# A gated conv block on one core: y_b's scalings ordered behind y_a's last evacuation, and T2 built pair by pair between the FFN's first products

## The chip, the core and the metric

The kernel runs on one core of one Trainium2 chip. The time is the device time of one execution in microseconds; lower is better. The core has a matrix engine (TensorE, PE in the profile), two elementwise engines (VectorE, DVE; ScalarE, ACT), a third (GpSimd, POOL), and a queue that issues loads (SyncE, SP). Each engine takes its instructions in the order that was compiled; an instruction that waits holds up all behind it on its engine.

## The reference

One layer of 1024 channels over 1024 time steps, all float32:

```python
h = rms_norm(x, norm_mix_g) * (1 + sc1) + sh1
b_s, c_s, v_s, v_c, gl_c, gate_br = split(h @ w_in)
y_a = (b_s * causal_dwconv3(c_s * v_s)) @ w_short_out
u = causal_dwconv31(v_c * sigmoid(gl_c)) + conv_conf_b
u = silu(layer_norm(u, conf_ln_g, conf_ln_b))
y_b = u @ w_conf_out
x = x + g1 * ((sigmoid(g_a) * y_a + sigmoid(g_b) * y_b) @ w_o)
h2 = rms_norm(x, norm_ffn_g) * (1 + sc2) + sh2
a, b = split(h2 @ w_ffn_in)                     # 2816 columns each
x = x + g2 * ((silu(a) * b) @ w_ffn_out)
out = rms_norm(x, final_norm_g)
```

The six modulations sc1, sh1, g1, sh2, sc2, g2 are silu(c) times w_ada, plus a bias.

## The kernel before

Channels lie on the 128 partitions, 8 blocks of them; time lies along the free dimension in two halves of 512. Each float32 product is made of three matmuls (`mm3`, L273 to L280): weight and activation are split in a high part (a cast on ACT, L203 for weights as `wh`, L308 or L316 for activations) and a remainder (a subtraction on DVE or POOL, L204 as `wl`, L309 or L317), and high x high, high x low, low x high are added up in PSUM. A stationary block of 128 x 128 with 512 columns is one matmul.

Weights come through a plan: `next_w` (L245) keeps three ready, each loaded by SP (L189) into one of five raw buffers and then split. A raw buffer also serves a modulation (`modulation`, L255): a load of w_ada, then one DVE reduction (L262). SP's load number n waits until the buffer of load n - 5 has been read to the end, by a remainder or a reduction.

Order around the first edit. y_a is computed output by output, 8 blocks of both halves (`col_block`, L692); each result is multiplied by its gate on DVE (L696), which also frees its PSUM bank. Meanwhile the LayerNorm of the 31-tap convolution gathers: `ln_square` (L642), `ln_rstd` (L654) with the two rows of 1/std `rl`, one for each half of time. `act_b(k, h)` (L673) then makes one operand of y_b: a scaling on DVE (L675), Silu on ACT (L676), and the split, zsh on ACT (L308) and zsl on DVE (L309). y_b is computed for one half at a time with all 8 outputs open at once (`row_blocks`, L358): for each k 8 x 3 matmuls, the last two k together. Its outputs take six banks of one pool, which y_a's results also use, and two of another. `next_b` (L679) makes the operand for the k after, and emits a modulation with it. At the end of a half each output is multiplied by its gate (L727), joined with y_a's and split (`join`, L714).

Order around the second edit. The FFN's products follow a seven-product scheme for 2 x 2 blocks (Winograd's form of Strassen's); `PRODUCTS` (L91) gives the order 1, 2, 6, 5, 7, 3, 4. The activations are the blocks b11, b12, b21, b22 of h2 (four pairs of channel blocks, two halves of time) and their sums T1 to T4. Products 1 and 2 need only the first half of time, 6 needs T2 = -(b11 - b12 + b22). For the first two groups of output columns the order is 1, 2 of the one, 1, 2 of the other (`in_order`, L820), and then the rest. `norm_2_start` (L901) sums the squares of the second half on PE; `rstd_end` (L330) makes 1/rms in three DVE operations; `h2_of` (L755) scales on DVE and adds the shift on ACT; `norm_2_last` (L777) does this for the second half of time, then builds T2, T1, T3, the split of b22 and T4, all emitted behind the four products.

The text of the program is not the order of the engines: a scheduler orders the emitted instructions on each engine by their dependences and its estimates, and `tc.issue_after(ins)` adds the rule that what is traced within it comes behind `ins` on the same engine. The weights of product 6 of the second group need four sums of raw weights on DVE first (L226 to L230).

Of the kernel before, what the change touches and what calls it, by code (L numbers as in the profile page):

```python
# [34 lines left out]
F32 = mybir.dt.float32  # L35
F32R = mybir.dt.float32r
AF = mybir.ActivationFunctionType
ALU = mybir.AluOpType
# [5 lines left out]
KC = D // P  # L44
# [61 lines left out]
def block_kernel(ctx: ExitStack, tc: tile.TileContext, xT, c, vecs, ada, w_first, w_plain, w_duals,  # L106
                 w_short, w_conf, w_o, w_fi, w_fo, w_last, outT):
    nc = tc.nc
# [9 lines left out]
    def close(*pools):  # L118
        for p, _ in reversed(pools):
            p.__exit__(None, None, None)  # L120
# [21 lines left out]
    def hl_tile(name, dt=F32R):  # L142
        return tp.tile([P, H], dt, tag="t", name=name)

    def s_tile(name, dt=F32):
        return hl_tile(name, dt)

    def g_tile(name):
        return gsp.tile([P, H], F32, tag="gs", name=name)

    def f32(t):
        return t.bitcast(F32)

    halves = (slice(0, H), slice(H, T))
# [18 lines left out]
    def col(base, k):  # L173
        return vec[:, base + k : base + k + 1]

    def modc(i):
        return mod[:, i : i + 1]
# [67 lines left out]
    def next_w(ahead=AHEAD):  # L245

        fetch(ahead + 1)
        return ready.pop(0)
# [6 lines left out]
    def modulation(i, raw=None):  # L255

        b = ADA_ORDER[i]
        if raw is None:
            raw = load(ada[i])
        else:  # L260
            nc.sync.dma_start(raw, ada[i])
        nc.vector.tensor_tensor_reduce(  # L262
            out=raw, in0=raw, in1=cs, scale=1.0, scalar=col(V_ADA, b),
            op0=ALU.mult, op1=ALU.add, accum_out=modc(b),
        )
# [16 lines left out]
    def col_block(w, act, hs, name):  # L282

        outs = [ps_tile(f"{name}{h}") for h in hs]
        for k in range(KC):
            mm3(outs, slice(k * P, k * P + P), w, [act[k][h] for h in hs], k == 0, k == KC - 1)
        return outs

    def product(banks, m, t, evac=None, between=None, y_tile=ps2_tile):

        w = next_w()
        b = {"1": "x", "6": "x", "7": "x", "4": "x", "2": "y", "5": "z", "3": "z"}[m]
        n = len(t)
        for p in range(2):
            if m in "125":
                banks[b, p] = (y_tile if b == "y" else ps_tile)(b)
            ps = banks[b, p]
            for k in range(n):
                c0 = (p * n + k) * P
                mm3([ps], slice(c0, c0 + P), w, [t[k]], m in "125" and k == 0, k == n - 1, m in "6734")  # L300
            if evac:
                evac(p, m, ps)
            if between and p == 0:
                between()

    def split(src, tile_of, name):
        hi, lo = tile_of(name + "h", dt=F32R), tile_of(name + "l", dt=F32R)
        nc.scalar.copy(hi, src)  # L308
        split.ins = nc.vector.tensor_tensor(lo, src, f32(hi), ALU.subtract).ins  # L309
        return hi, lo  # L310

    def t_pair(name):
        return hl_tile(name + "h"), hl_tile(name + "l")

    def t_split(src, hi, lo):
        nc.scalar.copy(hi, src)  # L316
        nc.vector.tensor_tensor(lo, src, f32(hi), ALU.subtract)  # L317

    def minus(out, a, b):

        nc.vector.scalar_tensor_tensor(out=out, in0=a, scalar=-1.0, in1=b, op0=ALU.mult, op1=ALU.subtract)
# [8 lines left out]
    def rstd_end(ss, eps, r, t, exp):  # L330

        nc.vector.scalar_tensor_tensor(out=t, in0=r, scalar=-0.5, in1=r, op0=ALU.mult, op1=ALU.mult)
        nc.vector.scalar_tensor_tensor(out=t, in0=ss, scalar=eps, in1=t, op0=ALU.add, op1=ALU.mult)
        nc.vector.scalar_tensor_tensor(out=r, in0=t, scalar=1.5, in1=r, op0=ALU.add, op1=ALU.mult)
        return r
# [123 lines left out]
    KH = KC // 2  # L459
    th = {m: [None] * KH for m in PRODUCTS}  # L460
    t2 = []
    for k in range(KH):
# [3 lines left out]
        t2 = hl_tile("t2", dt=F32)  # L466
# [164 lines left out]
    def ln_mean():  # L631
        mu = []
        for h in range(2):
            mps = ps_tile("mu")
            nc.tensor.matmul(mps, ones, tot[h], start=True, stop=True)
            nc.scalar.activation(tot[h], mps, AF.Copy, scale=1.0 / D)
            mu.append(tot[h])
        return mu
# [3 lines left out]
    def ln_square(j):  # L642
        cv.append(uc_tile(f"cv{j}", T))
        nc.sync.dma_start(cv[j], cv_dram[j])
        for h in range(2):
            nc.vector.tensor_tensor(cv[j][:, halves[h]], cv[j][:, halves[h]], mu[h], ALU.subtract)
            sq = g_tile("sq")
            nc.scalar.activation(sq, cv[j][:, halves[h]], AF.Square, scale=1.0 / 32.0)
            if j == 0:
                sqs[h] = sq  # L650
            else:
                nc.vector.tensor_tensor(sqs[h], sqs[h], sq, ALU.add)

    def ln_rstd(sqs):  # L654
        rs = []
        for h in range(2):
            var = ps_tile("var")
            nc.tensor.matmul(var, ones, sqs[h], start=True, stop=True)
            rs.append(rstd_start(var, eps2, f"rl{h}"))
        return [rstd_end(*r) for r in rs]  # L660
# [11 lines left out]

    def act_b(k, h):  # L673
        z = cv[k][:, halves[h]]
        nc.vector.tensor_tensor(z, z, rl[h], ALU.mult)  # L675
        nc.scalar.activation(z, z, AF.Silu, bias=col(V_LNB, k), scale=col(V_LNG, k))  # L676
        zs[k, h] = split(z, s_tile, "zs")

# [11 lines left out]
    ma = {}  # L690
    for j in range(KC):
        for h, ps in enumerate(col_block(next_w(), qT, (0, 1), "ya")):  # L692
            ga = g_tile("ga")
            nc.gpsimd.dma_start(ga, gate_dram["a", j][:, halves[h]])
            ma[j, h] = s_tile(f"ma{j}{h}")
            nc.vector.tensor_tensor(ma[j, h], ps, ga, ALU.mult)  # L696
        if j == 0:
            mu = ln_mean()
        if j < 5:
            for i in range((0, 1, 3, 5, 7)[j], (1, 3, 5, 7, 8)[j]):  # L700
                ln_square(i)
        if j == 5:
            rl = ln_rstd(sqs)
        if j == KC - 2:
            act_b(0, 0)
        if j < KC - 2:
            modulation(16 + j)
# [27 lines left out]
    x1 = [None] * KC  # L735
# [19 lines left out]
    def h2_of(k, h, r2, hi_lo=None):  # L755

        t = x1[k][:, halves[h]]
        nc.vector.scalar_tensor_tensor(out=t, in0=t, scalar=aff2[:, k : k + 1], in1=r2, op0=ALU.mult, op1=ALU.mult)
        if hi_lo:
            hi, lo = hi_lo  # L760
            nc.scalar.activation(hi, t, AF.Identity, bias=modc(24 + k))
            nc.vector.scalar_tensor_tensor(
                out=lo, in0=t, scalar=modc(24 + k), in1=f32(hi), op0=ALU.add, op1=ALU.subtract
            )
        nc.scalar.activation(t, t, AF.Identity, bias=modc(24 + k))
        return t


    ts = {m: [None] * (KC // 2) for m in PRODUCTS}
# [4 lines left out]
            ts["12"[k // KH]][k % KH] = hl = t_pair(f"h2{k}")  # L774
            h2_of(k, 0, r2, hl)

    def norm_2_last(r2):  # L777

        r2 = rstd_end(*r2)
        t2 = []  # L780
        for k in range(KH):
            h2_of(k, 1, r2)
            b22 = h2_of(k + KH, 1, r2)
            b11, b12 = (x1[k][:, s] for s in halves)
            nc.vector.tensor_tensor(b11, b11, b12, ALU.subtract)
            t2.append(hl_tile("t2", dt=F32))
            minus(t2[k], b11, b22)
            ts["6"][k] = t_pair("t2")
            t_split(t2[k], *ts["6"][k])
        for k in range(KH):  # L790
            ts["5"][k] = t_pair("t1")
            t_split(x1[k][:, halves[0]], *ts["5"][k])
        for k in range(KH):
            b12, b22 = x1[k][:, halves[1]], x1[k + KH][:, halves[1]]
            nc.vector.tensor_tensor(b12, b22, b12, ALU.subtract)
            ts["7"][k] = t_pair("t3")
            t_split(b12, *ts["7"][k])
        for k in range(KH):
            ts["3"][k] = t_pair("b22")
            t_split(x1[k + KH][:, halves[1]], *ts["3"][k])  # L800
        b21 = [x1[k + KH][:, halves[0]] for k in range(KH)]
        for k in range(KH):
            minus(b21[k], t2[k], b21[k])
        for k in range(KH):
            ts["4"][k] = t_pair("t4")
            t_split(b21[k], *ts["4"][k])
# [13 lines left out]
    in_order = [(d, m) for d in range(2) for m in "12"] + [(d, m) for d in range(2) for m in PRODUCTS[2:]]  # L820
# [83 lines left out]

    r2 = None
    product(in_banks[0], "1", ts["1"], in_evac(0), norm_2_start)
    for d, m in in_order[1:4]:
        in_product(d, m)
    norm_2_last(r2)
    close(*phase_1)  # L910
    raws.append(open_pool("raw_a", 1, side="right", stack=ctx)[1])
    x1ap = open_pool("x1a", 2, side="right", stack=ctx)[1]
# [13 lines left out]
    x1 = [x1ap.tile([P, T], F32, tag="x1", name=f"x1{j}") for j in range(2)]  # L926
# [184 lines left out]
```

## Time and profile before

| what | us |
|---|---|
| median of three runs | 1540.75 |
| lowest and highest of them | 1540.45, 1542.52 |
| profiled execution, its time | 1538.2 |
| profiled execution, span from the first to the last instruction | 1536.1 |
| mean granted TensorE clock in it | 0.987 |
| busy: PE, DVE, ACT, POOL | 1472.7, 1185.5, 617.3, 596.7 |

Times in the profile are counted from the span's start. A line of a timeline has the start, the length, the engine, the line of the kernel, the operation, what it writes and reads with their shapes, how many were merged, and in brackets the idle time before it and what ended it. A q behind an engine's name means its queue: SPq issues a DMA. PE's matmuls overlap, so a matmul of 0.39 us may start 0.23 us after the one before it. Outputs and operands go by name without a number: `yb` is any output of y_b, `x`, `y` and `z` are the PSUM banks of the FFN's products, `t2h` and `t2l` the split T2.

### The profile page before, as it was taken

The numbers are of one execution on the slowest core, as the hardware profiler recorded it, in microseconds if no ns is written. First come the engines' busy times: TensorE is split into PE (matmuls) and PEld (weight loads), VectorE is DVE, ScalarE is ACT, GpSimd is POOL, SyncE is SP. The second block draws the span as 40 slices with busy tenths as digits, with TensorE's granted clock in tenths as the row PEclk, the third lists the DMA queues.
The fourth block names the chain that finished last, engine by engine and source line by source line (L and its number), as shares of the span: only waits on it lengthen the run. The fifth ranks groups of instructions, "written<-read, shape, count | busy, mean of one in ns | idle before, by whom it ended". The sixth has DMA issues, their size and how long they took to land.

```text
span 1536.1 us, 17857 instructions
## 1 busy us (share of the span) xinstructions
PE 1472.7 (96%) x6466; PEld 1207.8 (79%) x6466; DVE 1185.5 (77%) x1559; ACT 617.3 (40%) x873; POOL 596.7 (39%) x493
## 2 busy tenths in 40 slices
PE   5899999999998999989999979999999999999996
PEld 3688887877886888868788858888888888888886
DVE  7987898999998972875876698876767765677756
ACT  5563433333333442343335354444444443221234
POOL 1326788798768883310121001100001116444005
PEclk9999999999999999999999989999999999999998
DMA  9432223223222159655754518544444449998403
GB/s 362 159 100 69 96 69 137 69 97 110 96 83 96 55 214 404 233 174 165 250 199 157 165 56 260 192 151 151 151 151 151 151 147 355 358 313 268 133 14 110
DMA packets 88024, 256.16 MB, mean 167 GB/s; under 512 B 10112, under 2 KB 12288, under 8 KB 87936
## 3 DMA queue, kind: packets, MB, share of 16 engines
q1 hardware_dynamic: 47248, 147.01, 28.5%
q0 software_dynamic: 36944, 95.44, 19.0%
q10 hardware_dynamic: 3744, 12.58, 2.0%
q8 instruction: 50, 0.82, 0.2%
q14 instruction: 38, 0.31, 0.1%
HBM read 188.41 MB, written 66.58 MB: 166 GB/s over the span
## 4 chain that ended last, share of the span: by engine, by line
PE 52%; issue 18%; DVE 15%; POOL 7%; DMA 6%; ACT 1%; SPq 0%; DVEq 0%; POOLq 0%; ACTq 0%
PE x L280 8%; PE x L277 8%; PE x L278 8%; DVE c L604 6%; PE z L277 4%; PE z L280 4%; PE z L278 4%; PE y L277 3%; PE y L280 3%; PE y L278 3%; POOL wl L204 2%; DMA raw<-in_ada 2%; DVE sc L496 1%; PE lead L278 1%; DVE ada L262 1%
## 5 line engine op out<-in xcount | busy, mean ns | idle before, releaser
L203 ACT CAST wh<-raw 128x1024 fp32r<-128x1024 f32 (+2 forms) x260 | 262.0, 1009 | 416.9 <-PE x L278 106.5
L204 POOL TENSOR_TENSOR wl<-raw,wh 128x1024 fp32r<-128x1024 f32 (+1 forms) x95 | 242.4, 2558 | 95.4 <-ACT wh L203 95.2
L204 DVE TENSOR_TENSOR wl<-raw,wh 128x1024 fp32r<-128x1024 f32 (+2 forms) x165 | 190.3, 1154 | 61.0 <-ACT wh L203 58.4
L604 DVE SCALAR_TENSOR_TENSOR c<-diff,vec,c 128x512 f32<-128x512 f32 x248 | 182.4, 750 | 3.7
L862 POOL DMA_DIRECT2D hid<-stage x71 | 37.8, 532 | 359.1 <-DVE stage L317 355.0
L280 PE MATMUL x<-th,wl 128*128 128x512 f32 x336 | 130.7, 389 | 0.0
L278 PE MATMUL x<-tl,wh 128*128 128x512 f32 x336 | 130.7, 389 | 0.0
L277 PE MATMUL x<-th,wh 128*128 128x512 f32 x336 | 130.7, 389 | 0.0
L604 DVE SCALAR_TENSOR_TENSOR c<-u,wsum,c 128x512 f32<-128x512 f32 x112 | 84.1, 751 | 2.0
L277 PE MATMUL x<-t2h,wh 128*128 128x512 f32 x184 | 73.8, 404 | 9.5 <-ACT wh L203 4.5
L280 PE MATMUL x<-t2h,wl 128*128 128x512 f32 x184 | 73.3, 399 | 4.3 <-POOL wl L204 4.0
L262 DVE CUSTOM_DVE_ANT_0 raw<-raw,cs,vec 128x1024 f32<-128x1024 f32 x24 | 35.0, 1462 | 51.0 <-DMA raw<-in_ada 47.1
L278 PE MATMUL x<-t2l,wh 128*128 128x512 f32 x184 | 73.4, 399 | 0.1
L280 PEld LDWEIGHTS x<-th,wl 128*128 128x128 f32 x336 | 63.1, 188 | 13.1
L278 PEld LDWEIGHTS x<-tl,wh 128*128 128x128 f32 x336 | 63.1, 188 | 13.1
L277 PEld LDWEIGHTS x<-th,wh 128*128 128x128 f32 x336 | 63.1, 188 | 13.1
L280 PE MATMUL z<-th,wl 128*128 128x512 f32 x168 | 65.5, 390 | 0.0
L277 PE MATMUL z<-th,wh 128*128 128x512 f32 x168 | 65.4, 389 | 0.0
L278 PE MATMUL z<-tl,wh 128*128 128x512 f32 x168 | 65.4, 389 | 0.0
L316 ACT CAST stage<-g 128x512 fp32r<-128x512 f32 x62 | 38.3, 620 | 58.9 <-DMA hid<-stage 28.4
L888 POOL DMA_DIRECT2D th<-hid x71 | 38.0, 535 | 54.3 <-PE x L280 28.8
L317 DVE TENSOR_TENSOR stage<-g,stage 128x512 fp32r<-128x512 f32 x62 | 42.5, 688 | 19.8 <-ACT stage L316 19.6
(811 smaller groups left out, 4096.0 us busy)
## 6 DMA issues: line engine op xcount, KB each, us to landing
hid<-stage POOLq DMA_DIRECT2D x71, 512.0 KB, 4.2
raw<-in_w_fi SPq DMA_DIRECT2D x50, 512.0 KB, 4.0
raw<-in_w_duals SPq DMA_DIRECT2D x48, 512.0 KB, 3.5
th<-hid POOLq DMA_DIRECT2D x71, 256.0 KB, 5.9
tl<-hid POOLq DMA_DIRECT2D x71, 256.0 KB, 5.9
ada<-in_ada SPq DMA_DIRECT2D x24, 512.0 KB, 7.6
raw<-in_ada SPq DMA_DIRECT2D x24, 512.0 KB, 4.6
raw<-in_w_fo SPq DMA_DIRECT2D x24, 384.0 KB, 6.0
```

The source lines that it names most:

```text
L203: nc.scalar.copy(wh, raw)
L204: lo = lo_engine.tensor_tensor(wl, raw, f32(wh), ALU.subtract)
L262: nc.vector.tensor_tensor_reduce(out=raw, in0=raw, in1=cs, scale=1.0, scalar=col(V_ADA, b), op0=ALU.mult, op1=ALU.add, accum_out=modc(b),)
L277: nc.tensor.matmul(ps, wh, xh, start=first, stop=False, skip_group_check=again)
L278: nc.tensor.matmul(ps, wh, xl, start=False, stop=False, skip_group_check=again)
L280: mm3.ins = nc.tensor.matmul(ps, wl, xh, start=False, stop=last, skip_group_check=again).ins
L316: nc.scalar.copy(hi, src)
L317: nc.vector.tensor_tensor(lo, src, f32(hi), ALU.subtract)
L496: nc.vector.scalar_tensor_tensor(out=sc[j], in0=p[:, s : s + T], scalar=col(V_SW + s * KC, j), in1=sc[j], op0=ALU.mult, op1=ALU.add)
L604: tap.ins = nc.vector.scalar_tensor_tensor(out=out, in0=src[:, s : s + H], scalar=wt, in1=acc, op0=ALU.mult, op1=ALU.add).ins
L862: nc.gpsimd.dma_start(hid_dram[key], s)
L888: nc.gpsimd.dma_start(t, hid_dram[key][:, s])
```

## The change

Two edits. First, each scaling of `act_b` that is traced after y_a's last product is ordered behind the DVE multiplication that evacuates that product; only the scaling of operand (0, 0), traced earlier, is not. Second, `norm_2_last` is cut in two: the three operations of 1/rms are emitted behind the first product, and the second half of h2 with T2 is emitted one pair of channel blocks at a time, the first three ahead of the second, third and fourth product, the fourth behind them. T1, T3, b22 and T4 follow as before. No operation is added, dropped or changed in size.

```diff
     def act_b(k, h):
         z = cv[k][:, halves[h]]
-        nc.vector.tensor_tensor(z, z, rl[h], ALU.mult)
+        with ExitStack() as order:
+            if (KC - 1, 1) in ma:
+                order.enter_context(tc.issue_after(ma["ins"]))
+            nc.vector.tensor_tensor(z, z, rl[h], ALU.mult)
         nc.scalar.activation(z, z, AF.Silu, bias=col(V_LNB, k), scale=col(V_LNG, k))
...
-            nc.vector.tensor_tensor(ma[j, h], ps, ga, ALU.mult)
+            ma["ins"] = nc.vector.tensor_tensor(ma[j, h], ps, ga, ALU.mult).ins
...
-    def norm_2_last(r2):
-
-        r2 = rstd_end(*r2)
-        t2 = []
-        for k in range(KH):
-            h2_of(k, 1, r2)
-            b22 = h2_of(k + KH, 1, r2)
-            b11, b12 = (x1[k][:, s] for s in halves)
-            nc.vector.tensor_tensor(b11, b11, b12, ALU.subtract)
-            t2.append(hl_tile("t2", dt=F32))
-            minus(t2[k], b11, b22)
-            ts["6"][k] = t_pair("t2")
-            t_split(t2[k], *ts["6"][k])
+    t2 = []
+
+    def norm_2_half(k, r2):
+
+        h2_of(k, 1, r2)
+        b22 = h2_of(k + KH, 1, r2)
+        b11, b12 = (x1[k][:, s] for s in halves)
+        nc.vector.tensor_tensor(b11, b11, b12, ALU.subtract)
+        t2.append(hl_tile("t2", dt=F32))
+        minus(t2[k], b11, b22)
+        ts["6"][k] = t_pair("t2")
+        t_split(t2[k], *ts["6"][k])
+
+    def norm_2_last():
+
         for k in range(KH):
             ts["5"][k] = t_pair("t1")
...
     product(in_banks[0], "1", ts["1"], in_evac(0), norm_2_start)
-    for d, m in in_order[1:4]:
+    r2 = rstd_end(*r2)
+    for i, (d, m) in enumerate(in_order[1:4]):
+        norm_2_half(i, r2)
         in_product(d, m)
-    norm_2_last(r2)
+    norm_2_half(KH - 1, r2)
+    norm_2_last()
```

## The prediction

> **What bounds the kernel now.** I read the page's shares first, then the waits of PE, then the order of time on PE, DVE, SP and ACT around the two edits.
>
> ```profile
> span 1536.1 us, 17857 instructions
> PE 1472.7 (96%) x6466; PEld 1207.8 (79%) x6466; DVE 1185.5 (77%) x1559; ACT 617.3 (40%) x873; POOL 596.7 (39%) x493
> ...
> 1300.00:1400.00 100.00, 100.00 (x443) 82.78 (x442) 70.69 (x92) 23.61 (x30) 45.38 (x86) 1.00 0.94 301
> ```
>
> PE is busy 96% of the span. In the third line, one stretch of 100 us late in the kernel, PE is busy all of it (second figure) at full granted clock, with the DMA engines at 0.94: 443 matmuls, 0.226 us each, so 24 of them (one k of y_b, one FFN product) take 5.42 us. The kernel ends when PE's list ends; only PE's holes are worth time. PE's longest waits at the two places:
>
> ```profile
> PE yb L277 <- DVE ma L696: 5.1, 1, 5.1
> PE x L277 <- ACT t2h L316: 4.5, 2, 3.4
> ```
>
> Each line: who waited for whom, total, times, longest. The first place in order of time, PE then DVE:
>
> ```profile
> 680.98 0.39 PE L277 MATMUL yb<-zsh,wh 128*128 128x512 f32 x1
> 689.82 0.80 PE L277 MATMUL yb<-zsh,wh 128*128 128x512 f32 x1 [5.08 <-DVE ma L696]
> 694.80 0.40 PE L277 MATMUL yb<-zsh,wh 128*128 128x512 f32 x1
> ...
> 674.64 1.28 DVE L262 CUSTOM_DVE_ANT_0 raw<-raw,cs,vec 128x1024 f32<-128x1024 f32 x1
> 678.86 1.28 DVE L696 TENSOR_TENSOR ma<-ya,ga 128x512 f32<-128x512 f32 x2
> 680.06 1.21 DVE L204 TENSOR_TENSOR wl<-raw,wh 128x1024 fp32r<-128x1024 f32 x1
> 681.79 3.09 DVE L675 TENSOR_TENSOR cv<-cv,rl1r 128x512 f32<-128x512 f32 x5
> 686.06 1.28 DVE L262 CUSTOM_DVE_ANT_0 raw<-raw,cs,vec 128x1024 f32<-128x1024 f32 x1 [1.17 <-DMA raw<-in_ada]
> 689.08 1.28 DVE L696 TENSOR_TENSOR ma<-ya,ga 128x512 f32<-128x512 f32 x2
> ...
> 681.30 0.33 SPq L189 DMA_DIRECT2D raw<-in_ada  x1
> ```
>
> y_b starts at 680.98; its fifth output needs the bank that y_a's last evacuation frees, and that product (689.08) stands in DVE's queue behind the normalization products (L675) and a modulation (L262) whose load SP issued only at 681.30, when the weight remainder of 680.06 gave its buffer back. The first 24 matmuls take 694.80 - 680.98 = 13.8 us instead of 5.4.
>
> The second place, the FFN's start, DVE, ACT, PE:
>
> ```profile
> 871.99 1.23 DVE L230 TENSOR_TENSOR raw<-raw 128x1024 f32<-128x1024 f32 x1 [0.66 <-DMA raw<-in_w_fi]
> 880.17 0.69 DVE L332 SCALAR_TENSOR_TENSOR r2t<-r2r 128x512 f32<-128x512 f32 x1
> 884.47 1.23 DVE L204 TENSOR_TENSOR wl<-raw,wh 128x1024 fp32r<-128x1024 f32 x1 [3.62 <-ACT wh L203]
> 908.56 1.22 DVE L204 TENSOR_TENSOR wl<-raw,wh 128x1024 fp32r<-128x1024 f32 x1
> 920.73 1.22 DVE L204 TENSOR_TENSOR wl<-raw,wh 128x1024 fp32r<-128x1024 f32 x1
> ...
> 889.31 1.04 ACT L203 CAST wh<-raw 128x1024 fp32r<-128x1024 f32 x1 [0.20 <-PE y L278]
> 918.56 1.04 ACT L203 CAST wh<-raw 128x1024 fp32r<-128x1024 f32 x1 [5.29 <-DVE raw L228]
> ...
> 889.06 0.39 PE L280 MATMUL y<-h27h,wl 128*128 128x512 f32 x1
> 892.86 1.22 PE L277 MATMUL x<-t2h,wh 128*128 128x512 f32 x2 [3.41 <-ACT t2h L316]
> 919.66 0.77 PE L277 MATMUL x<-t2h,wh 128*128 128x512 f32 x1 [4.54 <-ACT wh L203]
> 922.00 0.79 PE L280 MATMUL x<-t2h,wl 128*128 128x512 f32 x1 [0.30 <-DVE wl L204]
> ```
>
> The first four products end at 889.06; the next needs T2, begun at 880.17. From 880.17 to the weight sums of the second dual unit DVE is the bound: all its work in this stretch comes behind that start, and PE waits for it twice, 3.4 and 4.5 us.
>
> **The change, part by part.** No instruction is added or removed on any engine; what counts is the order. I take it from the order compiled for the changed kernel, and durations from rows above: a 512-wide DVE operation 0.60 to 0.66 (681.79: five in 3.09), a weight remainder 1.14 to 1.2, a modulation 1.28.
>
> *Part one, y_b.* In the new order DVE has the first scaling, the modulation of 674.64, both products of y_a's seventh block, a weight remainder, the first zsl, the next modulation, y_a's last two products, and only then the other scalings. With the modulation at 673.7 (its load was issued at 669.2, about 4.5 earlier), the remainder ends at 677.3 instead of 681.2. SP then issues the next load at 677.3; loads in this stage take
>
> ```profile
> 713.45 0.33 SPq L189 DMA_DIRECT2D raw<-in_ada  x1
> ...
> 712.19 1.22 DVE L204 TENSOR_TENSOR wl<-raw,wh 128x1024 fp32r<-128x1024 f32 x1 [2.92 <-ACT wh L203]
> 717.20 1.29 DVE L262 CUSTOM_DVE_ANT_0 raw<-raw,cs,vec 128x1024 f32<-128x1024 f32 x1 [3.78 <-DMA raw<-in_ada]
> 724.21 1.28 DVE L262 CUSTOM_DVE_ANT_0 raw<-raw,cs,vec 128x1024 f32<-128x1024 f32 x1 [4.58 <-DMA raw<-in_ada]
> 737.23 0.69 DVE L727 TENSOR_TENSOR gb<-yb,gb 128x512 f32<-128x512 f32 x1
> 737.98 0.50 PE L277 MATMUL yb<-zsh,wh 128*128 128x512 f32 x1 [0.84 <-DVE gb L727]
> 739.18 0.50 PE L277 MATMUL yb<-zsh,wh 128*128 128x512 f32 x1 [0.23 <-DVE gb L727]
> ```
>
> 3.75 (713.45 to 717.20) to 4.76 us (681.30 to 686.06). So the modulation runs at 682.1, y_a's last products end at 683.9 and 684.5, and the fifth output waits about 0.3 us, not 5.08. The second block's operand needs a scaling, Silu, cast and remainder after 684.5, about 0.7 each: ready at 687.5, where PE arrives at 686.7. PE then starts its third block at 692.7; before it was 694.80 + 5.42 = 700.2. That would be 7.5 us.
>
> I do not take 7.5, because the scalings are now between the weights on DVE. From 684.5 to the remainder that ran at 712.19 DVE has 15 scalings, 10 zsl, 4 remainders, 2 modulations: 25 x 0.6 + 4 x 1.14 + 2 x 1.28 = 22.1, plus some 1.2 of waits: 707.8, only 4.4 earlier. From there the loads are a chain: this remainder frees the buffer, a load, the modulation, the next remainder, a load (about 4.55), the modulation of 724.21. That is 707.8 + 1.1 + (3.75 to 4.76) + 1.28 + 1.14 + 4.55 = 719.6 to 720.6. Behind that modulation (1.28) the new queue has 13 operations of 0.6, one modulation and two remainders up to the seventh evacuation of y_b, 11.4: done at 732.3 to 733.3 against 737.9. PE, with y_b's first half done at 725.3, wants that bank at 729.4 and waits 2.9 to 3.9 us. The stall therefore returns, smaller, at the seam of the halves. Counted at the 49th matmul of the second half: before 739.2 + 27 x 0.226 = 745.4 (a second, 0.23 us wait ends at 739.18); after 732.8 + 30 x 0.226 = 739.6, plus 0.6 for the eighth bank or 1.7 if the clock drops, so 740.2 to 741.3. Part one: 4.1 to 5.2, taken 4.7; with both load times and the chain's error 3.2 to 6.2; 7.5 if the chain holds nothing up.
>
> The scalings also gate POOL's queue:
>
> ```profile
> 689.45 1.74 POOL L726 DMA_DIRECT2D gb<-gate_b  x3 [8.48 <-DVE cv L675]
> ```
>
> These gate loads take the buffers that the last scalings free; that now happens by 707.8, so the last of them is issued some 18 us later than at 689.45 and still some 13 us ahead of y_b's first evacuations at 721.
>
> Whether such a gap slows the clock:
>
> ```profile
> 472.08 0.50 PE L280 MATMUL x<-h00h,wl 128*128 128x512 f32 x1 [2.79 <-POOL wl L204]
> 487.39 0.50 PE L280 MATMUL x<-t2h,wl 128*128 128x512 f32 x1 [2.52 <-POOL wl L204]
> ...
> 475.00:476.00 1.00, 1.00 (x4) 0.51 0.00 0
> 488.00:489.00 1.00, 1.00 (x6) 1.00 0.65 172
> ```
>
> Columns of the last two: stretch, its length, PE busy (matmuls), granted clock, DMA share and GB/s. After 2.79 us of idle PE was still at half clock 3.5 us later (475 to 476), after 2.52 us it stayed at 1.00. Half the clock over some 3.5 us costs 1.7 us. Whether the seam's gap pays that I leave open; 4.7 is half way between. The Trainium skill, "TensorE: Matmul & The Clock Gate", Part 1, says that the array drops to half clock after an idle window of about 3.4 us, free-running. This trace disagrees on the limit: 2.79 us sufficed. By the page's figure alone the gap at the seam would often stay unpunished, and the sum below would be some 0.5 us better; I go by the row.
>
> *Part two, T2.* The three products that make 1/rms now start behind the weight sum of 871.99, at 873.2, instead of 880.17: 7.0 us earlier, in a stretch where DVE had room:
>
> ```profile
> 868.00:886.00 18.00, 18.00 (x78) 14.20 (x77) 10.49 (x12) 5.99 (x8) 0.00 (x0) 1.00 0.35 102
> ```
>
> DVE is busy 10.49 of these 18 us, and PE, busy all of them, needs nothing new from it there. From 880.17 to the remainder at 908.56 DVE took 28.4 us, 3.7 of them waiting (0.6 after 880.17 it was done, and went on at 884.47). In the new order the same stretch also holds two weight remainders that stood ahead of it and one small operation: 24.7 + 2 x 1.14 + 0.6 = 27.6. Its waits I follow pair by pair: the first two pairs are done at 886.4 without one; the third pair's cast stands on ACT behind the weight cast of 889.31, which waits for PE to leave the fourth product (PE's stop of 0.3 us ahead of that product's second half goes, since the sum's bank is read at 875.6; so 888.8). DVE comes there at 890.0 and waits 0.4; all waits 0.8. So the remainder of 908.56 runs at 873.2 + 27.6 + 0.8 = 901.6, 7.0 earlier. What follows up to the remainder of 920.73 is the same work in nearly the same order, with SP's loads issued as those remainders free buffers, so they move along: 913.7, and PE's first product with it at 914.9 instead of 922.00. Part two gives 7.1 us. PE's holes change shape: no 3.4 us at 889, but some 2.7 us at 893 to 895.6 for the fourth pair, and 3.0 us instead of 4.5 ahead of the second dual unit's weights. If these halve the clock, it costs little, since DVE sets the end of both products. If the new waits on ACT come to 3.7 as before, 7.1 - 2.9 = 4.2; with none, 7.9.
>
> *Sum.* From the seam to 868 and from 930 on the trace shows PE without a hole worth naming, so both shifts reach the end: 4.7 + 7.1 = 11.8 us. Against the profiled execution (span 1536.1, 1538.2 with what lies around it): span 1524.3, time 1526.4. The median of the runs is 2.5 above that execution, so 1540.75 - 11.8 = 1528.95.
>
> **The rivals.**
>
> *A: the loads do not hold up y_b.* If the chain through SP's loads runs ahead of need, part one gives its 7.5: 1540.75 - 14.6 = 1526.2. For it: the weights of the first blocks are 6 us ahead. Against: DVE waits for in_ada at 717.20 and 724.21 already now.
>
> *B: part one is given back at the seam.* If the seventh evacuation comes not 5 but 1 us earlier (the loads each take a microsecond more than the 4.76 and the clock halves), only part two is left: 1540.75 - 8.1 = 1532.7. For it: that evacuation is set by DVE and DMA, not by PE. Against: DVE's whole queue begins 4 to 6 us earlier.
>
> *C: T2's new place queues behind ACT.* The third and fourth pairs wait for the weight cast and hold DVE as long as the 3.62 us did: part two 4.2, in all 8.9: 1531.8. The 889.31 cast, which waits for PE whatever DVE does, speaks for it; that only the third cast meets it speaks against.
>
> *D, slower: the modulations' loads become the bound of y_b's second half too.* Load, modulation, remainder, one after the other, is 4.76 + 1.28 + 1.14 = 7.2 us a block against PE's 5.42. Over eight blocks that is 14.2 us more, less 4.7 and 7.1 gained: 2.4 slower, 1543.2. It decides from 1.5 us a block on (11.8 / 8). For it is the chain above; against it this row of the second half:
>
> ```profile
> 757.72 1.28 DVE L262 CUSTOM_DVE_ANT_0 raw<-raw,cs,vec 128x1024 f32<-128x1024 f32 x1 [1.30 <-DMA raw<-in_ada]
> ```
>
> DVE waits 1.3 us there, and PE has no wait: five buffers let two loads run ahead once the seam is passed.
>
> *E: no change.* If transfers and not PE pace what follows, being early only makes PE wait later: 1540.75. The row of 1300 to 1400, DMA at 0.94, is for it; that PE was busy 100.00 of 100 there is against.
>
> **How the numbers follow.** Forecast 0.55, A 0.12, B 0.12, C 0.10, D 0.07, E 0.04. The predicted time is the likeliest's, 1528.9. A measurement of this kernel can tell about 0.2% (3 us) from no change. The forecast, A, B and C are all faster by more: 0.89; E is the same, 0.04, and I leave 0.01 more for a remnant under 3 us: 0.05, which comes off B; D is the slower, 0.07. So faster 0.88. The range: best both upper ends, 7.5 + 7.9 = 15.4, 1525.3; worst the lower ends, 3.2 + 4.2 = 7.4, 1533.4; widened by the 2 us that the shown runs differ, on the slow side, 1525.0 to 1535.0. That leaves out D and E, and little else.
>
> **What will show it.** Right, if y_b's fifth output starts within 1 us of its fourth, DVE's last ma products come about 2.5 us after y_a's end, and a wait of PE for gb of 2 to 4 us stands at the seam; the T2 products begin without a wait, with a stop of some 2.7 us for the fourth pair; PE's wait for the second dual unit's weight is about 3 us. Wrong, if PE waits for wl or wh between blocks of y_b's second half (D), if the seam shows no wait over 1 us (A) or one over 5 (B), if DVE's T2 operations stand behind waits for ACT of over 2 us (C), or if PE shows new holes after the first dual unit (E).

## The result, and the profile after

| | kernel before | changed kernel |
|---|---|---|
| median of the runs, us | 1541.05 (4 runs, 1540.45 to 1542.52) | 1530.41 (4 runs, 1529.21 to 1531.64) |
| ratio | 1 | 0.993, 95% interval 0.9912 to 0.9947 |
| profiled execution: time, span, us | 1538.2, 1536.1 | 1529.94, 1528.0 |
| mean granted TensorE clock | 0.987 | 0.989 |

The changed kernel is 10.6 us faster by the medians; 11.8 were forecast. The two profiled executions differ by 8.1 us of span, because the second had lost time before it came to the edits: y_b begins at 682.79 us in it and at 680.98 in the other, and y_a, ahead of the first edit, began as much later already (592.28 and 590.47). So the two are compared from anchors, y_b's first matmul and the first one of the stage after it. Two lines of the changed kernel's page, and then who PE waited for (columns: total, times, longest):

```profile
span 1528.0 us, 17853 instructions
PE 1468.8 (96%) x6466; PEld 1205.1 (79%) x6466; DVE 1183.9 (77%) x1559; ACT 616.9 (40%) x873; POOL 597.2 (39%) x493
```

```profile
PE yb L277 <- DVE gb L730: 3.1, 2, 2.9
PE x L277 <- ACT wh L203: 2.8, 1, 2.8
PE x L277 <- ACT t2h L316: 2.3, 1, 2.3
...
PE yb L277 <- DVE ma L699: 0.8, 1, 0.8
```

The wait of 5.1 us for ma is down to 0.8, and a wait of 2.9 us for gb has come in its place, where it was 1.1 in two. The waits for t2h and for the second dual unit's wh went from 3.4 and 4.5 us to 2.3 and 2.8.

The anchors, in order of time on PE: the first product of the stage after y_b in the kernel before, then of the changed kernel y_b's start, the same product, and the first product with the second dual unit's remainder.

```profile
778.07 0.39 PE L277 MATMUL mix<-mg00h,wh 128*128 128x512 f32 x1
```

```profile
682.79 0.39 PE L277 MATMUL yb<-zsh,wh 128*128 128x512 f32 x1
...
777.05 0.39 PE L277 MATMUL mix<-mg00h,wh 128*128 128x512 f32 x1
...
913.82 0.80 PE L280 MATMUL x<-t2h,wl 128*128 128x512 f32 x1 [0.25 <-DVE wl L204]
```

y_b took 778.07 - 680.98 = 97.09 us before and 94.26 after: part one gave 2.8 us. From there to the product with the remainder it took 922.00 - 778.07 = 143.93 before and 136.77 after: part two gave 7.2. What follows took 614.1 and 614.2 us to the end of the span: both gains reach the end. 2.8 + 7.2, less the 1.8 lost before the edits and 0.1 behind them, is the 8.1 of the spans.

Where part one's gain stopped, in order of time: DVE, then SP, POOL and PE.

```profile
710.32 1.22 DVE L204 TENSOR_TENSOR wl<-raw,wh 128x1024 fp32r<-128x1024 f32 x1
715.95 1.28 DVE L262 CUSTOM_DVE_ANT_0 raw<-raw,cs,vec 128x1024 f32<-128x1024 f32 x1 [4.41 <-DMA raw<-in_ada]
723.05 1.28 DVE L262 CUSTOM_DVE_ANT_0 raw<-raw,cs,vec 128x1024 f32<-128x1024 f32 x1 [3.54 <-DMA raw<-in_ada]
734.95 0.68 DVE L730 TENSOR_TENSOR gb<-yb,gb 128x512 f32<-128x512 f32 x1
739.90 0.69 DVE L730 TENSOR_TENSOR gb<-yb,gb 128x512 f32<-128x512 f32 x1 [1.86 <-DMA gb<-gate_b]
...
711.57 0.33 SPq L189 DMA_DIRECT2D raw<-in_ada  x1
...
735.32 0.54 POOL L729 DMA_DIRECT2D gb<-gate_b  x1 [4.74 <-DVE mg10l L309]
...
735.68 0.50 PE L277 MATMUL yb<-zsh,wh 128*128 128x512 f32 x1 [2.90 <-DVE gb L730]
740.64 0.50 PE L277 MATMUL yb<-zsh,wh 128*128 128x512 f32 x1 [0.25 <-DVE gb L730]
```

The remainder at 710.32 gives its buffer back, SP issues the load at 711.57, DVE stands still for it until 715.95, and 3.5 us more for the next one: 8 us of idle DVE ahead of the evacuations of y_b's first half. The seventh (734.95) ends 2.9 us after PE wanted its bank. The eighth (739.90) waits for something else, its gate, which POOL could issue only at 735.32, when the remainder mg10l gave up the buffer.

### The profile page after: what moved, and what is told of

The parts are those of the page before. It is cut to its first block, busy times and chain, and to the rows that moved or that the text cites. A ratio compares the mean times of both kernels' runs of the same rounds, so it can differ in the third digit from the quotient of the medians.

```text
span 1528.0 us, 17853 instructions
## 1 busy us (share of the span) xinstructions
PE 1468.8 (96%) x6466; PEld 1205.1 (79%) x6466; DVE 1183.9 (77%) x1559; ACT 616.9 (40%) x873; POOL 597.2 (39%) x493
## 4 chain that ended last, share of the span: by engine, by line
PE 67%; DVE 15%; DMA 6%; POOL 5%; issue 5%; ACT 1%; SPq 0%; DVEq 0%; ACTq 0%; POOLq 0%
PE x L280 10%; PE x L278 9%; PE x L277 9%; DVE c L604 6%; PE z L278 5%; PE z L280 5%; PE z L277 5%; PE y L277 3%; PE y L278 3%; PE y L280 3%; POOL wl L204 3%; DMA raw<-in_ada 2%; PE mix L277 2%; PE mix L278 2%; PE mix L280 2%
```

## The experiments

Each ratio is to the kernel before, run in the same round on the same chip (its medians there: 1540.2 to 1541.4). y_b is the time from its first matmul to the first of the stage after; T2 is from there to the first product with the second dual unit's remainder, both from the profiled execution.

| kernel | median, us | ratio, 95% interval | y_b, us | T2, us |
|---|---|---|---|---|
| before (profile of the prediction) | | 1 | 97.09 | 143.93 |
| changed | 1530.41 | 0.993 (0.9912 to 0.9947) | 94.26 | 136.77 |
| e1_yb_only | 1538.51 | 0.9981 (0.9969 to 0.9993) | 94.45 | 143.91 |
| e2_t2_only | 1533.79 | 0.9959 (0.9946 to 0.9972) | 97.56 | 136.78 |
| e3_loads_to_mix | 1523.99 | 0.9897 (0.9881 to 0.9912) | 87.04 | 137.12 |
| e8_no_ada_loads | 1523.58 | 0.9881 (0.9862 to 0.9900) | 87.08 | 137.40 |
| e9_scalings_held | 1529.58 | 0.9925 (0.9908 to 0.9942) | 93.07 | 137.47 |
| e5_double_loads (one run) | 1541.75 | | 94.75 | 137.49 |
| e4_rms_early | 1531.75 | 0.9939 (0.9923 to 0.9954) | 94.47 | 137.13 |
| e6_remainders_on_pool | 1532.75 | 0.9944 (0.9926 to 0.9961) | 94.61 | 139.79 |
| e11_mix_rms | 1523.64 | 0.9897 (0.9878 to 0.9915) | 87.04 | 137.93 |
| e12_mix_halves | 1525.04 | 0.9900 (0.9883 to 0.9916) | 87.04 | 137.62 |

### Each part alone

The edit of e1_yb_only is the diff's first half, that of e2_t2_only its second.

> Part one alone: y_b's scalings ordered behind y_a's last evacuation, T2 as in the kernel before. Theory (the two parts add up, as the traces of before and after align): y_b's first wait shrinks from 5.1 to under 1 us, a wait for gb of about 3 us with the clock halved after it stands at the seam, and the kernel gains 2.8 us: ratio 0.998. The prediction's own size was 4.7 us: 0.997. Rival B (the seam gives it all back): within 0.5 us, 1.000. Rival A (the loads hold nothing up): 7.5 us, 0.995, and no wait over 1 us at the seam.

> Part two alone: T2 pair by pair between the first products, y_b's scalings as in the kernel before. Theory (independent parts): 7.1 us gained, ratio 0.9954; y_b's wait of 5.1 us for ma is back; in the FFN a wait of about 2.3 us for the fourth pair's t2h and one of about 2.8 us for the second dual unit's weight. Rival (the parts lean on each other, the FFN's gain needs y_b to be early): under 5 us, ratio 0.997 or more.

Part one alone gains 2.9 us by the ratio (0.0019 of 1540.8; 1.1 to 4.8 by the interval), part two alone 6.3 (4.3 to 8.3). Their columns show each part's stretch at the length of the changed kernel and the other's at that of the kernel before: the parts do not lean on each other. Rivals A and B for part one fall: the first would be 0.995, the second 1.000, and the interval leaves out both, the second narrowly. The wait of 2.9 us at the seam is against both too (A: none over 1 us, B: over 5).

### Do the loads make the seam?

e3_loads_to_mix takes the eight modulations out of y_b's first half:

```diff
-        modulation(24 + KC * h + k)
+        if h == 1:
+            modulation(24 + KC * h + k)
...
             mix(j, h)
+            if h == 0:
+                modulation(24 + j)
```

> The changed kernel with the eight modulations of y_b's first half (24 to 31) emitted one per output in the first half of the stage after it, where DVE waits for PE; the arithmetic is the same. Theory (a chain of buffer, load, modulation, remainder delays DVE, and with it y_b's seventh evacuation): the wait of 2.9 us at the seam goes below 1 us, the clock stays at 1.00 there, and about 4.9 us are gained on the changed kernel (2.9 of the wait and 2.0 of the half clock): ratio to the kernel before 0.990, some 1525.5 us. Rival (the queue of scalings on DVE alone sets the seam, not the loads): the wait stays above 2 us, ratio 0.993. Rival (the loads only collide one stage later): the seam closes but PE waits for weights among the mix outputs, ratio 0.993 or more.

y_b takes 87.04 us, which is its 384 matmuls at 0.227 us each: PE has no wait in it at all, nor among the mix outputs. The gain on the changed kernel is 7.2 us in y_b, more than the 4.9 expected, in part because the smaller waits at y_b's start go too (0.8 and 0.3), and so does the wait of the eighth bank. By the medians 6.4 us of it arrive, by the ratios 5.1. But this kernel removes DVE work (8 reductions) and loads together. e8_no_ada_loads keeps the work and removes only the loads:

```diff
-        modulation(24 + KC * h + k)
+        if h == 0:
+            nc.vector.tensor_tensor_reduce(
+                out=raw_tile(1024), in0=cs, in1=cs, scale=1.0, scalar=col(V_ADA, ADA_ORDER[24 + k]),
+                op0=ALU.mult, op1=ALU.add, accum_out=modc(ADA_ORDER[24 + k]),
+            )
+        else:
+            modulation(24 + KC * h + k)
```

> The changed kernel in which the eight modulations of y_b's first half keep their DVE reduction (cs times cs into the raw buffer) and lose their load; left out are those eight loads of w_ada, and with them the values of modulations 24 to 31. DVE's work is the same. The run with the modulations moved to the stage after took away DVE work and loads together; this one takes the loads alone. Theory (a chain of loads): DVE's waits for in_ada of 4.4 and 3.5 us ahead of the seam go, y_b's seventh evacuation comes some 8 us earlier, PE's wait at the seam goes below 1 us, and y_b takes under 89.5 us from its first matmul to the first of the stage after (94.3 in the changed kernel, 97.1 before); about 4.9 us gained, ratio 0.990. Rival (DVE's work, scalings and reductions, sets the seam): the wait stays at 2 us or more and y_b at 93 us or more, ratio 0.993.

DVE's waits from 675 to 735 us, in the changed kernel and then in this one:

```profile
DVE raw L262 <- DMA raw<-in_ada: 14.5, 5, 4.6
```

```profile
DVE ma L705 <- PE ya L280: 6.7, 1, 6.7
DVE raw L262 <- DMA raw<-in_ada: 4.1, 2, 3.6
DVE wl L204 <- ACT wh L203: 2.4, 1, 2.4
```

With as many reductions on DVE, of the same 1.28 us each, y_b is at 87.08 us and PE waits for nothing in it. In the changed kernel DVE stood 14.5 us for five loads; here it stands for PE (6.7 us, for y_a's last output): it is ahead instead of behind. What holds part one back is the loads, and not DVE's work. One reservation: without the loads the scheduler also sets some scalings a few places earlier on DVE.

e9_scalings_held goes at the start of that chain: the last five scalings leave the queue ahead of the remainder that frees the buffer.

```diff
             if (KC - 1, 1) in ma:
                 order.enter_context(tc.issue_after(ma["ins"]))
+            if "gb" in ma:
+                order.enter_context(tc.issue_after(ma["gb"]))
...
-            nc.vector.tensor_tensor(g, yb[o], g, ALU.mult)
+            ma["gb"] = nc.vector.tensor_tensor(g, yb[o], g, ALU.mult).ins
```

> The changed kernel with the last five scalings of the second half ordered behind the evacuation of y_b's eighth output of the first half; nothing else. They leave DVE's queue ahead of the weight remainder that gives the raw buffer to the next load. Theory (those scalings start the chain 5 x 0.6 = 3.0 us late): the remainder and all that follows come 3 us earlier, the wait of 2.9 us at the seam falls to about 1 us, the clock is not halved, 2 to 4 us gained on the changed kernel, ratio 0.9905 to 0.992. Rival (the chain is paced by the loads from further back, the scalings fill time in which DVE would wait): the seam's wait stays above 2 us, ratio 0.993. Rival (held back, they come too late for the second half): PE waits for zsh or zsl after the seam, ratio above 0.993.

In order of time, DVE, POOL and then PE:

```profile
706.69 1.23 DVE L204 TENSOR_TENSOR wl<-raw,wh 128x1024 fp32r<-128x1024 f32 x1
712.54 1.28 DVE L262 CUSTOM_DVE_ANT_0 raw<-raw,cs,vec 128x1024 f32<-128x1024 f32 x1 [4.62 <-DMA raw<-in_ada]
719.40 1.29 DVE L262 CUSTOM_DVE_ANT_0 raw<-raw,cs,vec 128x1024 f32<-128x1024 f32 x1 [4.43 <-DMA raw<-in_ada]
730.06 2.35 DVE L204 TENSOR_TENSOR wl<-raw,wh 128x1024 fp32r<-128x1024 f32 x2
732.46 0.69 DVE L732 TENSOR_TENSOR gb<-yb,gb 128x512 f32<-128x512 f32 x1
738.85 0.69 DVE L732 TENSOR_TENSOR gb<-yb,gb 128x512 f32<-128x512 f32 x1 [1.21 <-DMA gb<-gate_b]
...
728.63 0.54 POOL L731 DMA_DIRECT2D gb<-gate_b  x1 [31.30 <-DVE mg00l L309]
...
733.21 0.50 PE L277 MATMUL yb<-zsh,wh 128*128 128x512 f32 x1 [2.04 <-DVE gb L732]
739.60 0.50 PE L277 MATMUL yb<-zsh,wh 128*128 128x512 f32 x1 [1.14 <-DVE gb L732]
```

Here y_b began 1.0 us earlier than in the changed kernel, so the remainder is 2.6 us earlier against it, nearly the 3.0 expected. That advance is still whole at the second of the two modulations (719.40 against 723.05, 2.7 us with the later start taken off): the loads moved along with the buffer, as the chain says. DVE's two waits are 9.1 us in place of 8.0 only because one remainder of 1.14 us, which stood between them, now comes behind them.

The advance is lost behind the chain. The gate loads of y_b take buffers that the scalings free, and the five scalings held back did not free theirs: POOL issued the sixth gate at 728.63, behind the remainder mg00l (its wait in the row), and not at 710.59, behind a scaling, as in the changed kernel. That gate landed at 732.37, and the sixth evacuation followed at 732.46; two weight remainders, now ahead of it on DVE, would have held it as long. PE waits 2.0 us for it, and the eighth evacuation still waits for its own gate. y_b gains 1.2 us, little more than half of the least that was expected, and the medians (0.8 us apart) cannot tell it from nothing.

e5_double_loads puts two modulations to each operand of the first half and none into the second.

```diff
-        modulation(24 + KC * h + k)
+        if h == 0:
+            modulation(24 + 2 * k)
+            modulation(25 + 2 * k)
```

> The changed kernel with two modulations for each operand of y_b's first half and none in its second: the suspected cost doubled where the seam is, and taken from where it is hidden. Theory (a chain of buffer, load, modulation, remainder): with three loads a block through five buffers a block of y_b's first half takes 1.3 to 5.7 us longer than the 7.1 us measured between the modulations ahead of the seam, so PE waits for weights inside the first half (rival D's picture), and y_b takes 105 to 140 us instead of 94.3; the kernel is slower than before by 8 us or more. Rival (loads run ahead through the five buffers, DVE's order sets the seam): y_b within 3 us of 94.3.

```profile
666.98 0.77 PE L277 MATMUL ya<-q00h,wh 128*128 128x512 f32 x1 [4.90 <-DVE ma L701]
...
698.83 0.79 PE L277 MATMUL yb<-zsh,wh 128*128 128x512 f32 x1 [4.51 <-DVE ma L701]
...
691.80 1.29 DVE L262 CUSTOM_DVE_ANT_0 raw<-raw,cs,vec 128x1024 f32<-128x1024 f32 x1 [3.85 <-DMA raw<-in_ada]
696.88 1.28 DVE L262 CUSTOM_DVE_ANT_0 raw<-raw,cs,vec 128x1024 f32<-128x1024 f32 x1 [3.78 <-DMA raw<-in_ada]
```

This expectation missed: no weight of y_b is late, PE's wait at the seam is only 0.6 us, and y_b as a whole takes 94.75, which is what the rival had forecast for it. But the scheduler drew the added loads forward. Ten of the sixteen modulations run inside y_b's first half (six of eight in the changed kernel), and DVE's waits for loads stand mostly ahead of y_a's last evacuation: two modulations that wait for theirs come right before it (698.09, right behind the second), PE waits 4.5 us for it, and 4.9 for an earlier one inside y_a. The run is 11.3 us behind the changed kernel, and no faster than the kernel before. So the doubled loads did not press where they were meant to, and this run decides neither for the theory nor for the rival. It does show once more that a load hurts here when DVE waits for it ahead of an evacuation.

### What gives part two its gain?

e4_rms_early emits the three operations of 1/rms behind the first product, and all four pairs behind the fourth, as before:

```diff
-    for i, (d, m) in enumerate(in_order[1:4]):
-        norm_2_half(i, r2)
+    for d, m in in_order[1:4]:
         in_product(d, m)
-    norm_2_half(KH - 1, r2)
+    for i in range(KH):
+        norm_2_half(i, r2)
```

> The changed kernel with only the three operations of 1/rms emitted behind the first product; all four pairs of T2 are emitted behind the four products, as in the kernel before. Theory (the early start of DVE's list is the gain, and the scheduler interleaves the pairs by itself): within 1.5 us of the changed kernel, ratio 0.993. Rival (the pairs must be emitted between the products, or a weight remainder that waits for ACT holds DVE up again): 3 us or more of the 7.1 are lost, ratio 0.995 to 0.998, with a wait of DVE for wh of over 2 us behind the start of T2.

T2 takes 137.13 us, 0.4 more than with the pairs between the products and 6.8 less than before. DVE's order is nearly the same, since the scheduler interleaves the pairs by itself once 1/rms is there. The median is 1.3 us behind the changed kernel's and the intervals overlap. The early 1/rms is the gain; the pair by pair emission adds nothing to it that can be seen. Waits only change places: 1.3 us for t2h and 4.5 for wh, where the changed kernel has 2.3 and 2.8, with nearly the same end. That is what it looks like when DVE's list, and not one wait of PE, sets the end. DVE's windows from the start of 1/rms to the end of the second dual unit's remainder (stretch, its length, busy and instructions, granted clock, DMA share, GB/s), in the kernel before and in the changed one:

```profile
880.17:921.95 41.78, 38.13 (x56) 0.89 0.20 63
```

```profile
872.03:913.76 41.73, 41.16 (x59) 0.97 0.24 76
```

In the changed kernel DVE is busy for all but 0.6 of these 41.7 us. The stretch is as long as before; it only begins earlier.

e6_remainders_on_pool was to shorten that list, by giving three weight remainders to POOL, idle there:

```diff
+            lo = nc.gpsimd if early == 2 and m in "657" else eng
-            return split_w(a[{"6": "11", ...}[m]], n, (), eng)
+            return split_w(a[{"6": "11", ...}[m]], n, (), lo)
```

(`early` is 2 for the first dual unit alone.)

> The changed kernel with the weight remainders of the first dual unit's products 6, 5 and 7 on POOL, which is idle from 867 to 930 us, in place of DVE. Theory (DVE's list from the start of 1/rms to the second dual unit sets the end of both products): two remainders (2 x 1.14 us) leave the list ahead of the fourth pair of T2 and a third ahead of the second dual unit's sums; the wait of 2.3 us for the fourth pair goes, PE's first product with the second dual unit's weights comes 2.3 to 3.4 us earlier, ratio 0.9908 to 0.9915. Rival (the loads of the second dual unit set it: the wait for its weights grows by what the other shrinks): within 1 us of the changed kernel, ratio 0.993. Rival (a remainder on POOL takes 2.6 us and is late): PE waits for wl from POOL, ratio 0.993 or more.

T2 takes 139.79, 3.0 us longer than in the changed kernel. The reason stands in DVE's rows, with POOL's behind them:

```profile
878.91 2.77 DVE L788 TENSOR_TENSOR x<-x 128x512 f32<-128x512 f32 x1
...
886.60 2.88 DVE L762 SCALAR_TENSOR_TENSOR x<-x,aff,r2r 128x512 f32<-128x512 f32 x1
...
892.47 0.68 DVE L845 TENSOR_TENSOR g<-y,g 128x512 f32<-128x512 f32 x1
893.07 2.29 DVE L788 TENSOR_TENSOR x<-x 128x512 f32<-128x512 f32 x1
...
878.39 2.73 POOL L204 TENSOR_TENSOR wl<-raw,wh 128x1024 fp32r<-128x1024 f32 x1 [11.33 <-ACT wh L203]
886.52 2.41 POOL L204 TENSOR_TENSOR wl<-raw,wh 128x1024 fp32r<-128x1024 f32 x1 [5.39 <-ACT wh L203]
892.42 2.39 POOL L204 TENSOR_TENSOR wl<-raw,wh 128x1024 fp32r<-128x1024 f32 x1 [3.49 <-ACT wh L203]
```

Each time POOL works, one DVE operation of 0.68 to 0.74 us takes 2.3 to 2.9 and ends some 0.55 us behind POOL's. From one start on DVE to the next it is 2.7, 2.8 and 2.2 us in place of 0.6 to 0.7: 5.8 lost; three remainders taken away save 3 x 1.14 = 3.4. So DVE's list became 2.4 us longer, and T2 3.0 (2.2 to 3.0 against the 136.8 to 137.6 of the other kernels with the whole of part two): the test went the wrong way and still bears out that the list sets the end.

### The two together, and the stretch near 1310 us

e11_mix_rms joins e3's edit with e4's. e12_mix_halves joins e3's edit with this one:

```diff
-    for j in (4, 5, 2, 3, 6, 7):
-        nc.gpsimd.dma_start(x1[j], x1_dram[j])
+    for h in (1, 0):
+        for j in (4, 5, 2, 3, 6, 7):
+            nc.gpsimd.dma_start(x1[j][:, halves[h]], x1_dram[j][:, halves[h]])
```

> The modulations of y_b's first half moved to the stage after, together with 1/rms early and the four pairs of T2 emitted behind the four products. Theory (the seam's gain and the early 1/rms are independent, and the pair by pair emission adds nothing): within 1.5 us of the kernel with the moved modulations and the pairs between the products, ratio 0.988 to 0.991, no wait of PE inside y_b. Rival (the pairs' places matter once y_b is early): 3 us or more behind it, ratio 0.992 or more.

> The kernel with the moved modulations, and the reload of x ahead of the last products issued by halves of time, second halves first, which the first products write. In the profile of the kernel with the moved modulations DVE waited 7.0 us for that reload and PE 2.6 us behind it, near 1310 us, with the clock down for some 5 us; 4.2 us were lost there against the changed kernel. Theory (the reload's first pieces land too late when the DMA engines are full): the hole goes, the runs gather near 1522 us, ratio 0.987 to 0.989. Rival (it is chance in a stretch where the DMA share is 1.0 and more, and the pieces do not matter): runs spread from 1522 to 1528 as before, ratio 0.9897. Rival (twice as many issues on POOL's queue hold up the loads of th and tl): PE waits for th, ratio above 0.991.

e11_mix_rms stands where e3_loads_to_mix does, at 0.9897 both: the gains add, and the emission of the pairs makes no difference that can be seen. The three kernels with moved modulations cannot be told apart; by the medians they are 5 to 7 us faster than the changed kernel, and their intervals end below its ratio of 0.993 (its own begins at 0.9912, where theirs end). The row that e12 was made for, of e3_loads_to_mix:

```profile
1312.28 0.47 PE L277 MATMUL z<-th,wh 128*128 128x512 f32 x1 [2.64 <-issue]
...
1311.43 0.75 DVE L951 SCALAR_TENSOR_TENSOR x<-z,ng,x 128x512 f32<-128x512 f32 x1 [6.95 <-DMA x<-x_dram]
```

That wait of DVE for the reload of x is in every kernel, from 1.0 us in e4_rms_early over 4.4 in the changed kernel to 7.0 in e5_double_loads. At 6.9 us it cost PE 2.6 us in e3, and the granted clock was at a half for 3.4 us behind that. In e5, at 7.0, PE stood 1.4 us at that place. With the reload in halves it was 5.9 us, and PE waited 0.3; but e11_mix_rms, which has no halves, shows the same 5.9 and 0.3. The runs of e12 lie between 1522.6 and 1525.6, those of e11 between 1522.9 and 1525.4, those of e3 between 1521.9 and 1527.8. So PE stood long only where the wait was longest, but nothing shows that the halves shorten it; what made it 5.9 in one run and 6.9 in another stays open.

## Why the prediction was right, point by point

- **The stall at y_b's fifth output.** Forecast 0.3 us, measured 0.76, and 0.30 more for the second operand. PE began its third block 12.53 us after y_b's start (19.28 before): 6.75 us ahead, where 7.5 were worked out. Right.
- **The gain is given back at the seam through the chain of loads.** Less the 1.81 us of the later start, the remainder ran at 708.5 (forecast 707.8), the last modulation at 721.2 (719.6 to 720.6), and the seventh evacuation was done at 734.95 + 0.60 = 735.55, so at 733.7 (732.3 to 733.3). PE waited 2.90 us (2.9 to 3.9). e3 and e8 show the loads as the cause, by taking them away: no wait is left. That they form a chain is seen in the rows, and in e9, where an earlier remainder moved both loads.
- **The size of part one.** 4.7 us were forecast, 2.8 came, below the 3.2 given as its own lower end. Half of the 1.9 is the chain: the evacuation was 0.9 us later than the middle of its forecast. The other half lies behind the seam, in the step that gave the eighth bank 0.6 us, or 1.7 with the clock down. From the seventh evacuation to the 49th matmul of the half it took 744.41 - 735.55 = 8.9 us, and not 7.4 to 8.5:

```profile
744.41 0.39 PE L277 MATMUL yb<-zsh,wh 128*128 128x512 f32 x1
```

  The prediction had looked only at the gate loads that wait for scalings. The last ones wait for the split of y_b's own results; the eighth output's was issued at 735.32 and held DVE until 739.90.
- **Half the clock at the seam.** Left open with 1.7 us; the clock did fall (last section), but it cost little, because the eighth bank was late anyway. In e4_rms_early it did not fall, and from the end of the long wait to the stage after it took 41.05 us; in the changed kernel, at half clock, 777.05 - 735.68 = 41.37; in e6_remainders_on_pool, at half clock too, 41.02.
- **T2.** 7.1 forecast, 7.2 measured. On the kernel before's clock (1.02 us added, by the second anchor) 1/rms began at 873.05 (forecast 873.2), the remainder of 908.56 ran at 901.4 (901.6), the later one at 913.6 (913.7). PE's holes were 2.27 us (2.7) and 2.83 (3.0). The rows:

```profile
872.03 0.68 DVE L332 SCALAR_TENSOR_TENSOR r2t<-r2r 128x512 f32<-128x512 f32 x1
...
889.41 0.69 DVE L317 TENSOR_TENSOR t2l<-t,t2h 128x512 fp32r<-128x512 f32 x1 [0.42 <-ACT t2h L316]
...
900.38 1.22 DVE L204 TENSOR_TENSOR wl<-raw,wh 128x1024 fp32r<-128x1024 f32 x1
912.54 1.22 DVE L204 TENSOR_TENSOR wl<-raw,wh 128x1024 fp32r<-128x1024 f32 x1
...
894.54 0.74 PE L277 MATMUL x<-t2h,wh 128*128 128x512 f32 x2 [2.27 <-ACT t2h L316]
```

- The third pair's wait behind ACT is there with 0.42 us, forecast 0.4. Rival C needed over 2 us and falls.
- **Rivals D and E.** No weight is late in y_b's second half, so D falls. E is not seen between the edits and the end (614.1 and 614.2 us); in one profile of a kernel that comes to 1310 us earlier still, 4.2 us were lost there to a transfer.

By the sum the medians should differ by 11.8 us; the trace gives 10.0, and the medians 10.6. So the mechanism of both parts is as forecast, part two within 0.1 us; the total came out near because part one, too large by 1.9 us, is the smaller of the two, and the time (1530.41 for 1528.9) lies well inside a range of 10 us.

## What to carry to other kernels

Before moving a piece of elementwise work, list what waits behind it on its engine and which of these waits on a transfer: here seven microseconds hung on eight loads that were emitted where DVE had to wait for them ahead of an evacuation, and moving them one stage on, where DVE waits for PE, was worth as much as the larger half of the change. When an engine's list sets the end of a stage, start the list early; here the order inside it mattered little, and the waits that PE showed in it only traded places. Before holding work back, ask what it frees: the scalings held in e9 kept a gate's buffer. An idle engine is no free place for work until it is known what it shares with the busy one.

## What the runs showed of the hardware

A subtraction on POOL held up DVE's work in SBUF. In e6_remainders_on_pool, DVE operations with all tensor operands in SBUF ended only after POOL's subtraction had ended, three times of three, while one that reads PSUM (`g<-y,g`, 892.47) ran through in 0.68 us beside it. The Trainium skill, "GPSIMD Engine Reference", Key points, says that this engine shares its SBUF interfaces with VectorE and collides with its instructions that have two SBUF inputs. The rows above agree, and give the price here: 1.6 to 2.1 us of DVE for each POOL operation of 2.4 to 2.7.

The length of a hole does not by itself decide whether the clock falls behind it. In the changed kernel the clock was at a half behind holes of 2.90 and 2.83 us, and at 1.00 behind one of 2.27. But behind a hole of 2.30 us at that same place it was at a half in e9_scalings_held and at 1.00 in e2_t2_only; and behind the hole near 470 us it was at a half in the kernel before (2.79 us, the row of the prediction) and in e8_no_ada_loads (2.61), and at 1.00 in e12_mix_halves (2.79). So the prediction's reading that 2.79 us sufficed holds for that hole in that trace, and gives no limit.

What sorts the cases is a grid in time. The traces record the clock, and within each trace the stretches at half clock begin a whole number of steps of 3.413 us apart: in the changed kernel at 487.93, 737.10 and 911.18, which is 73 and 51 steps. Whether a step is at half clock goes by how long PE was idle in the step before it. Windows of PE cut on this grid (stretch, its length, busy and matmuls, granted clock, DMA share, GB/s), of the changed kernel and then of e9_scalings_held:

```profile
733.69:737.10 3.41, 1.42 (x6) 1.00 0.78 245
737.10:740.51 3.41, 3.30 (x8) 0.50 0.79 291
...
890.70:894.11 3.41, 1.58 (x7) 1.00 0.00 0
894.11:897.52 3.41, 2.84 (x11) 1.00 0.01 2
```

```profile
889.93:893.34 3.41, 1.11 (x4) 1.00 0.01 2
893.34:896.75 3.41, 3.28 (x9) 0.50 0.00 0
```

PE was idle 1.99 us of the first step, and the next was at half clock; 1.83 us, and the next was not; 2.30 us in e9, and the next was. Over all twelve traces, from 80 to 1500 us, there are 40 steps at full clock with 1.95 us or more of idle PE, and each was followed by half clock; of 36 steps with 1.2 to 1.94 us, one was (1.92 us). A hole of up to 3.9 us can lie across a line of the grid with less than 1.95 on either side, so where it falls is luck. The prediction quotes from the Trainium skill, "TensorE: Matmul & The Clock Gate", Part 1, an idle window of about 3.4 us, free-running. The steps of 3.413 us in these traces agree with its length; that the window must be idle throughout they do not bear out, since 1.95 us of it sufficed.
